# Last stage of a two-block transformer kernel: spilled columns, column order, look-ahead and engine of the elementwise work changed

## The chip, the cores and the metric

The kernel runs on one core of a Trainium2 chip. The metric is the device time of one execution in microseconds, as the median of several runs; lower is better.

## The reference, cut to what matters

The whole program is two transformer blocks on 512 tokens of width 1024. The change concerns the last part of the second block, a layer of 16384 experts (128 columns of 128), of which every token takes 8 x 16:

```
def block(xb):
    q = (xb @ w_query).reshape(T, 8, 2, 128)
    s = einsum('thpk,hpnk->thpn', q, sub_keys)
    top_s, top_i = top_k(s, 16)
    ...
    idx = ...                       # 16 experts per head and token
    gate = softmax(best_s)
    u = expert_u[idx]
    v = expert_v[idx]
    act = gelu(einsum('td,thkd->thk', xb, u))
    return einsum('thk,thkd->td', gate * act, v)
```

After it `x = x + gate2 * peer(...)` and a last rms norm with a weight follow.

## The kernel before, in words

Everything is kept in float32. A product is made of three matmuls on a high and a low part of each operand (`mm3`, L204). `unit` (L189) loads 128 x 1024 weights into one of three `raw` buffers with a DMA that SyncE issues, ScalarE copies them to `whi` (L200), and VectorE or another engine that is handed in subtracts (`wlo`, L201). `whi` and `wlo` have eight buffers each.

The first 128 tokens take their experts by gathering rows (`gather`, L1063): for each of 128 slots GpSimd issues an indirect DMA of 128 rows of 4 KB into one of four `grow` buffers, VectorE makes a dot product with `h2` (L1075), and later a second gathered row is accumulated into `acc0` (L1077). That is 256 gathers of 512 KB.

The other 384 tokens take all 16384 experts, by columns. For a column j, `expert_in` (L1054) multiplies the tokens with the column's `p_u` (24 matmuls of 384 columns) and takes the gelu into `act`. In the last stage, `experts_out` (L1212), `parts` multiplies `act` with the dense gates of the column (L1249), which an earlier stage left in DRAM (`gD`) and which come back as tiles of 4 columns, makes a high and a low part `wh`, `wl` (L1253, L1254), and `prod` multiplies these with the column's `p_v` (18 matmuls of 512 columns: 3 token tiles, 2 halves, `mm3`) into six banks that sum over all columns.

Of the 128 columns 64 (j < `NSPILL`) have their `act` made in the routing stage before, where TensorE waits for VectorE's top-k; they are stored in DRAM (`actD`, L1047) and loaded again in the last stage (`acts`, L1244, two buffers). They are *spilled*; the others are *fresh* and go through `expert_in` in the last stage. The last stage takes a fresh and a spilled column in turn (64, 0, 65, 1, ...). The fresh columns' `wlo` and all gate products are GpSimd's.

The program is written in this order, and then a list scheduler of the language puts each engine's instructions into an order of its own, by simulated times; buffers and semaphores are set after it. On an engine, and in SyncE's queue of loads, instructions then run strictly in that order, so that one which waits holds up those behind it.

Of the kernel before, what the change touches and what calls it, by code (L numbers as in the profile page):

```python
# [18 lines left out]
S = 512  # L19
# [7 lines left out]
NSPILL = 64  # L27
F1 = 4
# [13 lines left out]
# ---------------------------------------------------------------- constants of the shapes  # L42
# [55 lines left out]
# ---------------------------------------------------------------- layout of the inputs  # L98
# [72 lines left out]
# ---------------------------------------------------------------- the program  # L171
class Block:
# [15 lines left out]
    # ---- streams of weights  # L188
# [55 lines left out]
    def to_T(self, src, tt, kt, hh, hl, psp):  # L244
        """128 tokens' rows (features on the free axis) into the transposed pair."""
# [10 lines left out]
    def norm_T(self, np_, psp, tt, wrow):  # L256
        """rms norm of the residual's rows of token tile tt, weighted, into hT."""
# [38 lines left out]
    def post_norm(self, np_, tt, ps, wrow):  # L296
        """x += rms(ps) * w"""
# [8 lines left out]
    # ---- whole  # L306
    def run(self, upto=99):
# [7 lines left out]
        self.x = base.tile([128, NT, D], F32, name="x")  # L315
        nc.sync.dma_start(self.x[:, 0, :], a["x"][:128, :])
        self.hh = base.tile([128, 8, S], F32R, name="hh")
        self.hl = base.tile([128, 8, S], F32R, name="hl")
        self.hhF = self.hh.bitcast(F32)
# [3 lines left out]
        self.oml = base.tile([128, 4], F32, name="oml")  # L323
        self.psum = ctx.enter_context(tc.tile_pool(name="psum", bufs=1, space=PSUM))
# [15 lines left out]
    # ---- block 1, mixer  # L340
# [27 lines left out]
    def rope(self, T, psp, ps, C, Sg, dst, scale=1.0):  # L368
        """dst: a tile, or a pair of tiles that get one half of the partitions each"""
# [74 lines left out]
    def project_nsa(self, P, T, psp, cos, sin):  # L444
# [19 lines left out]
        # hl[:, h]: both parts of head h's queries, one on each half of the partitions;  # L464
        # hh[:, 4 * part + 2 * g + n]: one part of group g's keys, on both halves
# [120 lines left out]
    def attend(self, T, psp):  # L586
# [4 lines left out]
        for tt in range(NT - 1, -1, -1):  # L591
# [5 lines left out]
            # compressed keys  # L597
# [88 lines left out]
    # ---- block 1, conv ffn; the modulation of block 2 rides along  # L686
# [142 lines left out]
    def lower_bounds(self, pool):  # L829
        """the forget gates' lower bounds lb and 1 - lb, a column per head"""  # L830
# [12 lines left out]
    def hgrn(self, P, T, psp, ya, yb):  # L843
# [5 lines left out]
        # projections that the recurrence needs first  # L849
# [25 lines left out]
        # values and output gates, tokens on the partitions  # L875
# [41 lines left out]
    def hgrn_head(self, h, T, psp, tag, kT, qT, b, vv, ya, hm):  # L917
# [27 lines left out]
        # pairs of different token tiles; queries and keys decayed to the tiles' borders  # L945
# [75 lines left out]
    # ---- block 2, experts: token tile 0 gathers its rows, the other tiles take every expert  # L1021
    def peer(self):
# [3 lines left out]
        with ExitStack() as c0:  # L1026
            dr = c0.enter_context(tc.tile_pool(name="pdr", bufs=1, space=DRAM))
            self.actD = dr.tile([128, 128, n], F32, name="actD")
# [5 lines left out]
            with ExitStack() as c1:  # L1034
# [134 lines left out]
    def gates_dense(self, psp, sel, iota):  # L1169
        """the gate of every expert and token, tokens innermost, in DRAM"""  # L1170
# [41 lines left out]
    def experts_out(self):  # L1212
        tc, nc, a = self.tc, self.nc, self.a
        n = S - 128
        last = 4
        with ExitStack() as c0:
# [6 lines left out]
            early = {j: self.expert_in(T, psp.only("pre"), j, nc.gpsimd) for j in range(NSPILL, NSPILL + 3)}  # L1223
            acc = [[psp.tile([128, 512], F32, name="acc") for h in range(2)] for t in range(NT - 1)]
            fresh, spilled = list(range(NSPILL, 128)), list(range(NSPILL))
            order = []
            while fresh or spilled:
                if fresh:
                    order.append(fresh.pop(0))
# [126 lines left out]
```

## Time and profile before

| | |
|---|---|
| runs | 2371.37, 2372.2, 2373.32 us, median 2372.2 |
| span of the profiled execution | 2374.4 us (the page has no time of its own beside it) |
| TensorE busy | 2250.5 us (95%) |
| VectorE busy | 1732.7 us (73%) |
| ScalarE busy | 954.2 us (40%) |
| GpSimd busy | 1191.4 us (50%) |
| last stage | from about 1497 us to the end |

Busy times are sums over stages with different limits, so shares of the whole span tell little of one stage. DVE is VectorE, ACT is ScalarE, POOL is GpSimd, SPq is SyncE's queue that issues loads; PE is TensorE and PEld its weight loads. A matmul's duration in the profile is longer than its share of the pipe, since matmuls overlap; the pace is read from one start to the next. DMA share is the mean busy share of 16 DMA engines.

### The profile page before, as it was taken

The numbers are of one execution on the slowest core, as the hardware profiler recorded it, in microseconds if no ns is written. First come the engines' busy times: TensorE is split into PE (matmuls) and PEld (weight loads), VectorE is DVE, ScalarE is ACT, GpSimd is POOL, SyncE is SP. The second block draws the span as 40 slices with busy tenths as digits, with TensorE's granted clock in tenths as the row PEclk, the third lists the DMA queues.
The fourth block names the chain that finished last, engine by engine and source line by source line (L and its number), as shares of the span: only waits on it lengthen the run. The fifth ranks groups of instructions, "written<-read, shape, count | busy, mean of one in ns | idle before, by whom it ended". The sixth has DMA issues, their size and how long they took to land.

```text
span 2374.4 us, 32466 instructions
## 1 busy us (share of the span) xinstructions
PE 2250.5 (95%) x11849; PEld 1974.4 (83%) x11849; DVE 1732.7 (73%) x2873; ACT 954.2 (40%) x1540; POOL 1191.4 (50%) x811
## 2 busy tenths in 40 slices
PE   7998999999999999999998999899999999999996
PEld 6786878888889888798998999788888788888885
DVE  4347557886425487546599999488888899888898
ACT  4225444333326433433333599423333333333331
POOL 3234110000002233312468898578788888888886
PEclk9998999999999999999999999999999999999998
DMA  7323006765223211143344466899889899989985
GB/s 250 109 66 115 11 5 226 242 213 195 93 76 119 89 63 46 66 145 106 130 132 158 137 242 248 318 317 335 314 308 317 309 319 324 319 315 308 328 304 197
DMA packets 190480, 469.56 MB, mean 198 GB/s; under 512 B 19056, under 2 KB 87536, under 8 KB 190192
## 3 DMA queue, kind: packets, MB, share of 16 engines
q1 hardware_dynamic: 153456, 333.25, 41.2%
q0 software_dynamic: 36864, 134.23, 16.0%
q8 instruction: 93, 1.52, 0.3%
q14 instruction: 67, 0.55, 0.1%
HBM read 422.31 MB, written 39.85 MB: 195 GB/s over the span
## 4 chain that ended last, share of the span: by engine, by line
PE 55%; DVE 16%; DMA 11%; issue 8%; POOL 7%; ACT 3%; SPq 1%; DVEq 0%; POOLq 0%; ACTq 0%
PE b L206 15%; PE b L207 15%; PE b L208 15%; DMA grow<-in_p_v_dram,eid 4%; DMA grow<-in_p_ur_dram,eid 3%; POOL grow L1072 3%; PE b L1203 3%; DVE wlo L201 2%; DVE wl L1254 2%; POOL wlo L201 2%; DVE grow L1075 1%; DMA raw<-in_p_v_dram 1%; PE b L656 1%; DVE acc L1077 1%; ACT gst L1204 1%
## 5 line engine op out<-in xcount | busy, mean ns | idle before, releaser
L206 PE MATMUL b<-hh,wlo 128*128 128x384 f32 (+2 forms) x1872 | 663.1, 355 | 13.8 <-POOL wlo L201 7.3
L207 PE MATMUL b<-hl,whi 128*128 128x384 f32 (+2 forms) x1872 | 661.3, 354 | 3.6 <-DVE hl L288 3.4
L208 PE MATMUL b<-hh,whi 128*128 128x384 f32 (+2 forms) x1872 | 659.4, 353 | 0.0
L201 POOL TENSOR_TENSOR wlo<-raw,whi 128x1024 fp32r<-128x1024 f32 x143 | 359.2, 2521 | 514.6 <-ACT whi L200 500.8
L200 ACT ACTIVATE whi<-raw 128x1024 fp32r<-128x1024 f32 (+1 forms) x405 | 425.6, 1054 | 441.0 <-PE b L208 182.3
L201 DVE TENSOR_TENSOR wlo<-raw,whi 128x1024 fp32r<-128x1024 f32 x262 | 373.8, 1429 | 212.0 <-ACT whi L200 207.0
L206 PEld LDWEIGHTS b<-hh,wlo 128*128 128x128 f32 x1872 | 354.3, 190 | 45.7 <-POOL wlo L201 8.8
L207 PEld LDWEIGHTS b<-hl,whi 128*128 128x128 f32 x1872 | 355.8, 190 | 33.6 <-DVE hl L288 3.8
L208 PEld LDWEIGHTS b<-hh,whi 128*128 128x128 f32 x1872 | 355.0, 190 | 30.1 <-issue 0.4
L206 PE MATMUL b<-whi,wl 128*128 128x512 f32 x768 | 308.4, 402 | 43.7 <-DVE wl L1254 43.7
L207 PE MATMUL b<-wlo,wh 128*128 128x512 f32 x768 | 305.3, 398 | 0.0
L208 PE MATMUL b<-whi,wh 128*128 128x512 f32 x768 | 304.2, 397 | 0.0
L1075 DVE CUSTOM_DVE_ANT_0 grow<-grow,h 128x1024 f32<-128x1024 f32 x128 | 211.3, 1668 | 33.1 <-DMA grow<-in_p_ur_dram,eid 33.0
L1077 DVE SCALAR_TENSOR_TENSOR acc<-grow,gact,acc 128x1024 f32<-128x1024 f32 x127 | 216.0, 1701 | 22.5 <-DMA grow<-in_p_v_dram,eid 20.5
L1072 POOL DMA_INDIRECT grow<-in_p_v_dram,eid x128 | 193.4, 1511 | 75.1 <-DVE acc L1077 39.8
L1072 POOL DMA_INDIRECT grow<-in_p_ur_dram,eid x128 | 196.1, 1532 | 65.8 <-DVE gact L1075 41.0
L206 PEld LDWEIGHTS b<-whi,wl 128*128 128x128 f32 x768 | 147.5, 192 | 80.6 <-DVE wl L1254 50.9
L206 PE MATMUL b<-whi,hl 128*128 128x512 f32 (+1 forms) x464 | 181.6, 392 | 4.4 <-DVE hl L254 2.3
L208 PE MATMUL b<-whi,hh 128*128 128x512 f32 (+1 forms) x464 | 180.1, 388 | 0.0
L207 PE MATMUL b<-wlo,hh 128*128 128x512 f32 (+1 forms) x464 | 180.0, 388 | 0.0
L208 PEld LDWEIGHTS b<-whi,wh 128*128 128x128 f32 x768 | 148.1, 193 | 31.9
L207 PEld LDWEIGHTS b<-wlo,wh 128*128 128x128 f32 x768 | 148.3, 193 | 29.6
(296 smaller groups left out, 3093.6 us busy)
## 6 DMA issues: line engine op xcount, KB each, us to landing
raw<-in_p_u_dram SPq DMA_DIRECT2D x128, 512.0 KB
raw<-in_p_v_dram SPq DMA_DIRECT2D x128, 512.0 KB
raw<-in_w_adaT_dram SPq DMA_DIRECT2D x48, 512.0 KB
gD<-gst SPq DMA_DIRECT2D x48, 512.0 KB
raw<-in_w_up_dram SPq DMA_DIRECT2D x44, 512.0 KB
raw<-in_w_t_dram SPq DMA_DIRECT2D x32, 512.0 KB
gtf<-gD SPq DMA_DIRECT2D x16, 768.0 KB
gt<-gD SPq DMA_DIRECT2D x16, 768.0 KB
```

The costliest lines, as they stand in the source:

```text
L200: nc.scalar.activation(hi, raw, AF.Copy)
L201: (eng or nc.vector).tensor_tensor(lo, raw, hi.bitcast(F32), op=ALU.subtract)
L206: mm(out, al, bh, start=start, stop=False)
L207: mm(out, ah, bl, start=False, stop=False)
L208: mm(out, ah, bh, start=False, stop=stop)
L656: nc.tensor.matmul(po[:, i, :], pT[:, b, :], self.vv[:, b, 128 * br + 64 * g:128 * br + 64 * g + 64], start=b == 0, stop=b == tt)
L1072: nc.gpsimd.indirect_dma_start(out=g, out_offset=None, in_=rows[n], in_offset=bass.IndirectOffsetOnAxis(ap=self.eid[:, s:s + 1], axis=0))
L1075: nc.vector.tensor_tensor_reduce(g, g, self.h2, 1.0, 0.0, ALU.mult, ALU.add, act[:, s:s + 1])
L1077: nc.vector.scalar_tensor_tensor(self.acc0, g, act[:, s:s + 1], self.acc0, op0=ALU.mult, op1=ALU.add)
L1203: nc.tensor.matmul(ps[:, i, :], A[:, i, :], B[:, i, :], start=True, stop=True)
L1204: nc.scalar.activation(st.rearrange("p j t -> p t j")[:, 4 * t4:4 * t4 + 4, :], ps, AF.Copy)
L1254: nc.vector.tensor_tensor(wl, act, wh.bitcast(F32), op=ALU.subtract)
```

## The change

All of it is in `experts_out`, in the number of the columns that the routing stage spills, and in the order in which the base pool's tiles are made; comments and docstrings go as well, by which lines shift by up to two, and by four to five in `experts_out`.

- Spilled columns are the even ones, fresh the odd ones; the last stage takes 0, 1, 2, ... `actD` is half as long.
- Gate tiles hold 8 columns: 16 loads of 1536 KB instead of 32 of 768 KB.
- `parts` is written two columns ahead of `prod` (`AHEAD = 2`).
- The fresh columns' `wlo` and all gate products are VectorE's; GpSimd keeps the gathers' issues and small work at the end.
- `acts` has three buffers instead of two.
- In the base pool `x` comes behind `hh` and `hl`, which changes addresses.

```diff
+AHEAD = 2
...
-        self.x = base.tile([128, NT, D], F32, name="x")
-        nc.sync.dma_start(self.x[:, 0, :], a["x"][:128, :])
-        self.hh = base.tile([128, 8, S], F32R, name="hh")
...
+        self.hh = base.tile([128, 8, S], F32R, name="hh")
+        self.hl = base.tile([128, 8, S], F32R, name="hl")
+        self.hhF = self.hh.bitcast(F32)
+        self.x = base.tile([128, NT, D], F32, name="x")
+        nc.sync.dma_start(self.x[:, 0, :], a["x"][:128, :])
...
-            self.actD = dr.tile([128, 128, n], F32, name="actD")
+            self.actD = dr.tile([NSPILL, 128, n], F32, name="actD")
...
-                            act = self.expert_in(self.gpool or Q, psp, j, nc.gpsimd, "ga" if self.gpool else "act")
+                            act = self.expert_in(self.gpool or Q, psp, 2 * j, nc.gpsimd, "ga" if self.gpool else "act")
...
-            early = {j: self.expert_in(T, psp.only("pre"), j, nc.gpsimd) for j in range(NSPILL, NSPILL + 3)}
+            early = {j: self.expert_in(T, psp.only("pre"), j, nc.vector) for j in (1, 3, 5)}
...
-                g, jj = j // 4, j % 4
+                g, jj = j // 8, j % 8
...
-                    gts[g] = T.tile([128, 12, 4, 32], F32, name="gt" if g < NSPILL // 4 else "gtf")
+                    gts[g] = T.tile([128, 12, 8, 32], F32, name="gt")
...
+                if j % 2 == 0:
+                    act = T.tile([128, n], F32, name="acts", bufs=3)
+                    nc.sync.dma_start(act, self.actD[j // 2])
+                elif j in early:
+                    act = early.pop(j)
+                else:
+                    act = self.expert_in(T, psp, j, nc.vector)
                 v = self.unit(a["p_v"][j])
...
-                nc.gpsimd.tensor_tensor(act.rearrange("p (c t) -> p c t", t=32), act.rearrange("p (c t) -> p c t", t=32),
+                nc.vector.tensor_tensor(act.rearrange("p (c t) -> p c t", t=32), act.rearrange("p (c t) -> p c t", t=32),
...
-            for n_, j in enumerate(order[:-last]):
-                p = parts(j)
+            ready = [parts(j) for j in range(AHEAD)]
+            for j in range(128 - last):
+                ready.append(parts(j + AHEAD))
+                p = ready.pop(0)
```

The scheduler leaves every engine's order as it was up to the last stage. In it, TensorE's order before is this (a number at a name is the buffer's; `b4` and `b5` are the banks of `expert_in`, `b0` to `b7` else the sums; `wl_16586` belongs to the gelu of `b4_16557`, `wl_16696` to that of `b5_16667`):

```order
L208 MATMUL b4_16557<-hh_66,whi_16553 128x384
L206 MATMUL b5_16667<-hh_66,wlo_16664 128x384
...
L208 MATMUL b5_16667<-hh_66,whi_16663 128x384
L206 MATMUL b0_13317<-whi_16547,wl_16586 128x512
...
L208 MATMUL b7_13322<-whi_16615,wh_16622 128x512
L206 MATMUL b4_16774<-hh_66,wlo_16771 128x384
...
L206 MATMUL b0_13317<-whi_16657,wl_16696 128x512
```

The first `...` stands for the rest of 24 matmuls, the second for 36 of two columns, the third for the rest of 5. And now, at the same depth (`wl_16454` belongs to the product before `b4_16524`, `wl_16559` to `b4_16524`):

```order
L207 MATMUL b4_16524<-hh_68,wlo_16521 128x384
...
L209 MATMUL b4_16524<-hh_68,whi_16520 128x384
L207 MATMUL b0_13317<-whi_16448,wl_16454 128x512
...
L209 MATMUL b7_13322<-whi_16485,wh_16490 128x512
L207 MATMUL b5_16631<-hh_68,wlo_16628 128x384
...
L209 MATMUL b5_16631<-hh_68,whi_16627 128x384
L207 MATMUL b0_13317<-whi_16553,wl_16559 128x512
```

The products of an expert are no longer in pieces of 19, 24 and 5 but in 24s, each followed by 36 of two columns, and a column's first product has moved from behind the next expert to behind two columns and the next expert.

VectorE's order in the same place before (`acc0` rows are the gather's):

```order
L201 TENSOR_TENSOR wlo_16765<-raw_16762,whi_16764 128x1024
L1077 SCALAR_TENSOR_TENSOR acc0_8232<-grow_16220,gact_13198,acc0_8232 128x1024
L1077 SCALAR_TENSOR_TENSOR acc0_8232<-grow_16287,gact_13198,acc0_8232 128x1024
L1254 TENSOR_TENSOR wl_16586<-act_16582,wh_16585 128x384
L1254 TENSOR_TENSOR wl_16623<-acts_16619,wh_16622 128x384
L201 TENSOR_TENSOR wlo_16833<-raw_16830,whi_16832 128x1024
```

and now:

```order
L1079 SCALAR_TENSOR_TENSOR acc0_8232<-grow_16302,gact_13198,acc0_8232 128x1024
L1245 TENSOR_TENSOR act_16549<-act_16549,gt_16161 128x384
L1079 SCALAR_TENSOR_TENSOR acc0_8232<-grow_16305,gact_13198,acc0_8232 128x1024
L1250 TENSOR_TENSOR wl_16559<-act_16549,wh_16558 128x384
L1250 TENSOR_TENSOR wl_16598<-acts_16588,wh_16597 128x384
L202 TENSOR_TENSOR wlo_16701<-raw_16698,whi_16700 128x1024
L202 TENSOR_TENSOR wlo_16736<-raw_16733,whi_16735 128x1024
L1079 SCALAR_TENSOR_TENSOR acc0_8232<-grow_16370,gact_13198,acc0_8232 128x1024
L202 TENSOR_TENSOR wlo_16769<-raw_16766,whi_16768 128x1024
```

The gate product (L1245) and the fresh column's `wlo` (here `wlo_16736`) have come into VectorE's queue, between the gathered rows, of which it still takes four per two columns.

## Rows read from the trace of the kernel before

**Rows 1.** Stretches of the last stage: busy time by engine, clock, DMA share, GB/s
```profile
core 0: us, PE busy (x) PEld busy (x) DVE busy (x) ACT busy (x) POOL busy (x), PEclk, DMA share, GB/s
1515.00:2315.00 800.00, 760.40 (x3566) 663.43 (x3565) 692.12 (x609) 265.74 (x367) 650.44 (x419) 0.98 0.91 317
```
**Rows 2.** Timeline of TensorE: start us, duration us, instruction
```profile
1802.29 0.39 PE L208 MATMUL b<-whi,wh 128*128 128x512 f32 x1
...
1807.73 0.39 PE L208 MATMUL b<-whi,wh 128*128 128x512 f32 x1
...
1807.96 0.34 PE L208 MATMUL b<-hh,whi 128*128 128x384 f32 x1
...
1812.73 0.34 PE L208 MATMUL b<-hh,whi 128*128 128x384 f32 x1
```
**Rows 3.** Groups of instructions on TensorE, 1515 to 2315 us
```profile
line engine op names shapes xcount | busy us, mean ns | idle before us <-releasers
L206 PE MATMUL b<-whi,wl 128*128 128x512 f32 x724 | 290.2, 401 | 36.8 <-DVE wl L1254 36.8
...
L206 PE MATMUL b<-hh,wlo 128*128 128x384 f32 x465 | 158.1, 340 | 2.8 <-POOL wlo L201 2.8
```
**Rows 4.** Waits from 1500 us to the end: total us, times, longest
```profile
PE b L206 <- DVE wl L1254: 43.7, 21, 6.9
```
**Rows 5.** Timelines of VectorE and GpSimd, two places
```profile
1787.84 2.73 DVE L1254 TENSOR_TENSOR wl<-act,wh 128x384 fp32r<-128x384 f32 x1
1790.49 0.55 DVE L1254 TENSOR_TENSOR wl<-acts,wh 128x384 fp32r<-128x384 f32 x1
...
1808.63 1.21 DVE L201 TENSOR_TENSOR wlo<-raw,whi 128x1024 fp32r<-128x1024 f32 x1
1809.79 1.32 DVE L1077 SCALAR_TENSOR_TENSOR acc<-grow,gact,acc 128x1024 f32<-128x1024 f32 x1
...
1787.58 2.57 POOL L201 TENSOR_TENSOR wlo<-raw,whi 128x1024 fp32r<-128x1024 f32 x1
...
1807.77 1.78 POOL L1072 DMA_INDIRECT grow<-in_p_v_dram,eid  x1 [0.16 <-issue]
1809.86 0.94 POOL L1072 DMA_INDIRECT grow<-in_p_v_dram,eid  x1 [0.30 <-DVE wlo L201]
```
**Rows 6.** Groups of instructions on VectorE, 1515 to 2315 us
```profile
L1075 DVE CUSTOM_DVE_ANT_0 grow<-grow,h 128x1024 f32<-128x1024 f32 x125 | 206.8, 1672 | 33.1 <-DMA grow<-in_p_ur_dram,eid 33.0
L201 DVE TENSOR_TENSOR wlo<-raw,whi 128x1024 fp32r<-128x1024 f32 x118 | 195.6, 1660 | 21.3 <-ACT whi L200 21.2
L1077 DVE SCALAR_TENSOR_TENSOR acc<-grow,gact,acc 128x1024 f32<-128x1024 f32 x111 | 190.8, 1719 | 15.9 <-DMA grow<-in_p_v_dram,eid 14.1
L1254 DVE TENSOR_TENSOR wl<-act,wh 128x384 fp32r<-128x384 f32 x62 | 66.3, 1069 | 26.4 <-ACT wh L1253 20.9 <-ACT whi L200 3.0 <-issue 2.5
L1254 DVE TENSOR_TENSOR wl<-acts,wh 128x384 fp32r<-128x384 f32 x61 | 54.6, 895 | 6.6 <-ACT wh L1253 6.6
L1075 DVE DVE_READ_ACCUMULATOR2_ANT gact<- 128x1 f32 x124 | 9.5, 77 | 0.0
```
**Rows 7.** One line of VectorE, the gather's dot product: duration ns min/median/max
```profile
L1075 DVE CUSTOM_DVE_ANT_0 grow<-grow,h x128: 1207/1217/4919, 1503.7 to 2319.7; 128x1024 f32<-128x1024 f32 x128
```
**Rows 8.** Waits of SyncE's queue from 1500 us to the end
```profile
SPq L1244 <- DVE wl L1254: 235.3, 57, 10.4
...
SPq L192 <- POOL wlo L201: 171.7, 37, 6.3
```
**Rows 9.** Two stretches of 100 us in the stage, columns as in rows 1
```profile
1500.00:1600.00 100.00, 91.77 (x425) 80.03 (x425) 68.99 (x69) 31.46 (x45) 69.36 (x47) 0.97 0.94 331
...
1900.00:2000.00 100.00, 97.00 (x468) 85.53 (x468) 90.86 (x79) 33.48 (x46) 83.90 (x54) 1.00 0.94 327
```
**Rows 10.** DMA queues from 1500 us to the end: packets, MB, share of 16 engines
```profile
q1 hardware_dynamic: 86672, 136.86, 45.4%
q0 software_dynamic: 36705, 133.65, 43.2%
```
**Rows 11.** Timeline of VectorE at the start of the stage
```profile
1518.35 0.78 DVE L1254 TENSOR_TENSOR wl<-act,wh 128x384 fp32r<-128x384 f32 x1 [13.44 <-ACT wh L1253]
```
**Rows 12.** Waits from 2300 us to the end
```profile
PE b L206 <- DVE wl L1254: 7.5, 2, 6.9
```

More of the change, by code (lines that the diff above doesn't have):

```diff
@@ L314, in run @@
         nc.vector.memset(self.ones, 1.0)
-        self.x = base.tile([128, NT, D], F32, name="x")
-        nc.sync.dma_start(self.x[:, 0, :], a["x"][:128, :])
-        self.hh = base.tile([128, 8, S], F32R, name="hh")
-        self.hl = base.tile([128, 8, S], F32R, name="hl")
-        self.hhF = self.hh.bitcast(F32)
         self.mod = base.tile([128, 48], F32, name="mod")
@@ L1222, in experts_out @@
             g2 = self.gate_row(P, psp.only("u"), 40, "g2")
-            early = {j: self.expert_in(T, psp.only("pre"), j, nc.gpsimd) for j in range(NSPILL, NSPILL + 3)}
+            early = {j: self.expert_in(T, psp.only("pre"), j, nc.vector) for j in (1, 3, 5)}
             acc = [[psp.tile([128, 512], F32, name="acc") for h in range(2)] for t in range(NT - 1)]
[L1225 to L1229, printed above, removed]
-                if len(spilled) * (128 - NSPILL) > len(fresh) * NSPILL or not fresh:
-                    if spilled:
-                        order.append(spilled.pop(0))
@@ L1241, in parts @@
-                v = self.unit(a["p_v"][j])
-                if j < NSPILL:
-                    act = T.tile([128, n], F32, name="acts", bufs=2)
-                    nc.sync.dma_start(act, self.actD[j])
-                elif j in early:
-                    act = early[j]
-                else:
-                    act = self.expert_in(T, psp, j, nc.gpsimd)
-                nc.gpsimd.tensor_tensor(act.rearrange("p (c t) -> p c t", t=32), act.rearrange("p (c t) -> p c t", t=32),
+                                      self.gD[:, :, 256 * g:256 * g + 256].rearrange("c i n -> i c n"))
@@ L1255, in parts, with prod @@
                 return v, wh, wl
-            def prod(n_, t, v, wh, wl, halves=(0, 1)):
+            def prod(j, t, v, wh, wl, halves=(0, 1)):
                 tok = slice(128 * t, 128 * t + 128)
@@ L1260, in prod @@
                     c = slice(512 * h, 512 * h + 512)
-                    self.mm3(acc[t][h], wh[:, tok], wl[:, tok], v[0][:, c], v[1][:, c], n_ == 0, n_ == 127)
+                    self.mm3(acc[t][h], wh[:, tok], wl[:, tok], v[0][:, c], v[1][:, c], j == 0, j == 127)
             def finish(tt, src):
@@ L1277, in experts_out @@
             done = 0
-            for n_, j in enumerate(order[:-last]):
-                p = parts(j)
+            ready = [parts(j) for j in range(AHEAD)]
+            for j in range(128 - last):
+                ready.append(parts(j + AHEAD))
+                p = ready.pop(0)
                 for t in range(NT - 1):
-                    prod(n_, t, *p)
-                goal = min(257, 257 * (n_ + 1) // GBY)
+                    prod(j, t, *p)
+                goal = min(257, 257 * (j + 1) // GBY)
                 _advance(gather, goal - done)
@@ L1285, in experts_out @@
             _advance(gather, 999)
-            ps = [parts(j) for j in order[-last:]]
+            ready += [parts(j) for j in range(128 - last + AHEAD, 128)]
             finish(0, [self.acc0[:, :512], self.acc0[:, 512:]])
@@ L1289, in experts_out @@
                 for h in range(2):
-                    for i, p in enumerate(ps):
+                    for i, p in enumerate(ready):
                         prod(128 - last + i, t, *p, halves=(h,))
```

1 line of the change is left out of this document (removed).

## The prediction

> **What bounds the kernel now.** I read the stretches first, since one core runs four stages with different limits. The change moves no instruction ahead of the last stage, so only the time from about 1497 us on matters; the rest is taken as it is. There [rows 1], the 800 us from 1515 to 2315 are a steady state in which three resources are near full together: TensorE busy 760, VectorE 692, the DMA engines at a share of 0.91 (317 GB/s). GpSimd is at 650, ScalarE at 266. A share of 95% on TensorE says little, so I next work out what its matmuls need.
>
> The pace is read from starts [rows 2]. From 1802.29 to 1807.73 lie 24 steps of 512-wide matmuls, 0.2267 us each; from 1807.96 to 1812.73 lie 27 steps of 384-wide ones, 0.1767 us. The stretch holds 2170 of the first and 1396 of the second (three lines of nearly equal count each [rows 3]): 491.9 + 246.7 = **738.6 us of work in 800**. So 61.4 us are lost. Idle waits are 36.8 + 2.8 = 39.6 of them [rows 3]; the other 22 go with a mean granted clock of 0.98 [rows 1], that is, mostly 2.4 GHz with pieces at 1.2 after waits. That is all that can be won in the stretch.
>
> Next, who ends those waits. Nearly all of the idle is one sort: the first product of a column (L1261) waits for its `wl` [rows 4]. Its making is ScalarE's gelu, the product with the gate (L1249, GpSimd), ScalarE's copy `wh` and VectorE's `wl`. Two things make it late. First, TensorE's order gives every second column little room: as the order section shows, only the 24 matmuls of the next expert, 24 x 0.1767 = 4.2 us, lie between the last matmul behind `wl_16586` and its use; the other column has 41 matmuls, 36 x 0.2267 + 5 x 0.1767 = 9.0 us. Second, VectorE jams. The rows of one place show it [rows 5]: `wl` took 2.73 us at 1787.84 with GpSimd's 2.57 us subtraction beside it, and 0.55 at 1790.49 without one. The subtraction `wlo` took 1.21 and the accumulation 1.32 while GpSimd issued a gather; the issue does not slow them. The means over the stretch, 1672, 1660, 1719, 1069 and 895 ns [rows 6], against a median of 1217 for the gather's dot product [rows 7], tell that this is common.
>
> Last, the queue that issues loads: SyncE stood 235.3 us in total at the load of `acts` until `wl` set its buffer free, and 171.7 at loads of `raw` until GpSimd's `wlo` did [rows 8]. Behind a load that stands, all later ones stand too.
>
> **The change, part by part.**
>
> *GpSimd's work to VectorE.* In the stretch GpSimd loses about 59 subtractions and 123 gate products; VectorE gains them. With nobody beside it I price its work at the undisturbed durations: 125 dot products x 1.217 = 152; 125 reads of the accumulator x 0.077 = 10 [rows 6]; 118 + 59 = 177 subtractions x 1.21 = 214; 111 accumulations x 1.32 = 147; 123 `wl` x 0.55 = 68; 123 gate products of the same 128x384 shape, taken like `wl`, 68. Sum **659 us**, against 206.8 + 195.6 + 190.8 + 66.3 + 54.6 + 9.5 = 724 now. The added 139 us are more than paid by the jams that go. The gate product is not shown on VectorE; its ends are 0.55 (as `wl`) and 1.21 (as the 1024-wide subtraction), 81 us more and 740 in all. I take 0.55, the same size and two inputs.
>
> The Trainium skill, "Perfetto Trace Analysis", section "Optimizing Scalar/DVE Operations", speaks against this part: a saturated VectorE may be relieved by ScalarE or even GpSimd, which is what the kernel before does; the same section warns that the two share a read port, so that it might not help. The rows of group 5 side with the warning; by the rule alone the sum is that of rival 4.
>
> *Parts two columns ahead.* TensorE's new order is 24 matmuls for an expert, 36 for two products, 24, 36. Between the last matmul behind `wl_16559` and its use lie 36 + 24 matmuls, 12.4 us, against 4.2 and 9.0. Gelu, product, copy and `wl` follow within that even if VectorE is some us late. The cover for this is the weights' eight buffers; no third column of loads is needed beyond them.
>
> *`acts` with three buffers instead of two* takes part of the 235.3 us of standing out of SyncE's queue, and raw buffers come free with VectorE's 1.21 instead of GpSimd's 2.57 us. Both let loads start earlier, and what is then late is the DMA itself.
>
> *What loads can give.* The same bytes at the pure matmul pace need a share of 0.91 x 800 / 738.6 = 0.986. The best hundred microseconds in the stage show 0.94 [rows 9], with 0.92 of PE busy in one and 0.97 at clock 1.00 in the other. I take 0.94 as what better supplied queues reach all along: 800 x 0.91 / 0.94 = 774.5 us.
>
> *Gate tiles of 8.* Two loads of 768 KB become one of 1536 KB, with runs of 1 KB instead of 512 B: 24576 packets instead of 32 x 12 x 128 = 49152. Their price lies in [rows 10]: GpSimd's queue, nearly all 4 KB rows, moved 133.65 MB in 43.2%, 3.094 MB per percent. At that rate the other queue's 136.86 MB would be 44.2%, not 45.4: all short packets together cost 1.2% of 874 us, 10 us. Half of that, 5 us, is the gain (ends 0 and 10). So 774.5 - 5 = **769.5**, a gain of 30.5. The Trainium skill, "DMA: Bandwidth & Descriptors", section "Specifications", puts line rate at 512 B and above; by it this term would be 0, not 5.
>
> *TensorE's own side* would give less time: the better of the hundred-us rows is 97% busy [rows 9], 738.6 / 0.97 = 761.4. The later of the two, 769.5, is the forecast for the stretch.
>
> *Start.* The first product now is a spilled column that needs gate tile and `acts`; before, a fresh one, whose `wl` came at 1518.35 [rows 11]. Three gate products and one more `wh`/`wl` precede it on VectorE, 3 x 0.55 + 0.55 + 0.5, and its load follows the tile's: 0 to 5 us, taken as 2.
>
> *End.* TensorE waits up to 6.9 us there for the last columns' `wl` [rows 12]. Behind VectorE's last gathered rows it can stay or go: 0 to -7, taken as -4.
>
> *Spilled columns even, natural order, base pool:* the same 64 columns are spilled with the same loads and stores, only others; addresses move. 0, as VectorE's median of 1217 ns over four rotating buffers shows no place that is slower; ends 0 and 2 us either way.
>
> Sum: -30.5 + 2 - 4 = -32.5. The profiled execution's span is 2374.4 us, and 2341.9 comes of it. The median of the runs is 2372.2, 2.2 below the span, so **2340 us**.
>
> **The rivals.**
>
> 1. *The DMA stays where it is.* Four gather buffers and three raw buffers are unchanged, and 0.91 may be their limit. Then only the gate tiles and the end count, 5 + 4 - 2: 2365. For it: 0.91 is a mean over 800 us; against it: SyncE's standing [rows 8] is time with free engines. 0.14.
> 2. *All waits go.* The stretch falls to 738.6, with start 0 and end -7: -68, 2304. Against it: the share of 0.986. 0.08.
> 3. *VectorE's queue takes the place of GpSimd's (slower).* Everything that feeds TensorE now stands in one order with the gathered rows. Its waits in the stretch are 33.1 + 15.9 for rows, 21.3 + 26.4 + 6.6 for ScalarE's copies [rows 6], 103 in all. With 659 of work it fills 762; at 800 the change loses, so it decides at waits of 141, a third more. If they double, 659 + 206 = 865, less 2 at the ends: 2372 + 63 = 2435; half more gives 2384. Loads that start earlier speak against it. 0.11.
> 4. *The moved work keeps its stretched durations*, the skill's rule of above: 724 + 59 x 1.66 + 123 x 0.98 = 943 on VectorE, 143 more than the stretch: 2515. Only if the jams were not GpSimd's; [rows 5] speak against it. 0.03.
> 5. *Gains and new waits cancel*, within 0.2% (5 us, what a measurement of this kernel can tell from no change). 0.07.
>
> **How the numbers follow.** My forecast, 2315 to 2355, holds 0.57. Faster by over 0.2%: 0.57 + 0.14 + 0.08 = 0.79; same 0.07; slower 0.14. The range 2310 to 2372 leaves out rivals 3 and 4, most of 2 and half of 5. It takes in the ends of gate product, tiles, start and end.
>
> **What would show it.** VectorE's `wlo` and dot product near 1.21 us in the mean, the gate product at 0.55; idle of TensorE before `wl` below 10 us in the steady state; a DMA share of 0.94 or more; clock near 1.00; no SyncE wait on GpSimd. Wrong would be: means that stay above 1.5 us; VectorE over 95% busy with TensorE still waiting for `wl`; a DMA share of 0.91 with raw loads as the last wait (rival 1).

## The result, and the profile after

The changed kernel takes **2302.99 us** (median of four runs, 2300.91 to 2311.13) against 2372.76 us (2371.37 to 2382.8) of the kernel before, run beside it: a ratio of 0.9706 [0.9682, 0.9731], 69.8 us less. The prediction was 2340 with a range from 2310 to 2372; the time lies 7 us below the range, at the price of rival 2 (2304). The profiled execution is the longest of the four, 2311.13 us with a span of 2309.4.

The changed kernel's stretches of the last stage, columns as in [rows 1]:

```profile
1515.00:2215.00 700.00, 697.32 (x3355) 614.31 (x3356) 569.94 (x738) 250.10 (x343) 301.89 (x223) 0.99 0.94 340
1600.00:1700.00 100.00, 100.00 (x487) 88.46 (x486) 83.03 (x107) 35.79 (x49) 44.26 (x33) 1.00 0.96 348
2000.00:2100.00 100.00, 100.00 (x486) 88.28 (x485) 81.90 (x107) 37.11 (x51) 44.93 (x32) 1.00 0.92 338
```

From 1600 on TensorE is never without work and the granted clock is 1.00; [rows 1] had 95% and 0.98. The DMA share went from 0.91 to 0.94, the bytes from 317 to 340 GB/s.

The changed kernel's waits of TensorE, 1500 us to the end (total us, times, longest); they answer to [rows 4, 12]:

```profile
PE b L207 <- DVE wl L1250: 13.1, 1, 13.1
PE b L207 <- DVE wlo L202: 2.8, 1, 2.8
```

Both happen once, at the start of the stage. The 39.6 us of idle in the steady state [rows 3] are gone, and so is the wait at the end.

VectorE's groups in the changed kernel, 1515 to 2215 us, columns as in [rows 6]:

```profile
L202 DVE TENSOR_TENSOR wlo<-raw,whi 128x1024 fp32r<-128x1024 f32 x166 | 200.5, 1220 | 23.7 <-ACT whi L201 23.4
L1079 DVE SCALAR_TENSOR_TENSOR acc<-grow,gact,acc 128x1024 f32<-128x1024 f32 x111 | 142.0, 1279 | 4.4 <-DMA grow<-in_p_v_dram,eid 3.5
L1077 DVE CUSTOM_DVE_ANT_0 grow<-grow,h 128x1024 f32<-128x1024 f32 x111 | 133.8, 1219 | 2.2 <-DMA grow<-in_p_ur_dram,eid 2.0
L1245 DVE TENSOR_TENSOR acts<-acts,gt 128x384 f32<-128x384 f32 x60 | 33.2, 553 | 3.6 <-DMA acts<-actD 3.6
L1250 DVE TENSOR_TENSOR wl<-acts,wh 128x384 fp32r<-128x384 f32 x59 | 32.6, 552 | 5.5 <-ACT wh L1249 5.5
L1250 DVE TENSOR_TENSOR wl<-act,wh 128x384 fp32r<-128x384 f32 x58 | 32.1, 553 | 8.0 <-ACT wh L1249 8.0
L1245 DVE TENSOR_TENSOR act<-act,gt 128x384 f32<-128x384 f32 x55 | 30.7, 557 | 82.7 <-ACT act L1062 82.6
```

The means are what single undisturbed instructions were before [rows 5, 7]: 1220 ns for `wlo`, 1279 for the accumulation, 1219 for the dot product and 553 for the fresh column's `wl`, against 1660, 1719, 1672 and 1069 [rows 6]. The gate product, new on VectorE, takes 553 and 557. VectorE has taken over a third kind of work and is busy 81% of the stretch instead of 87%. The 82.6 us in the last row are spare time: the gelu it waits for follows TensorE.

SyncE's queue, 1500 us to the end (compare [rows 8]):

```profile
SPq L193 <- DVE wlo L202: 343.0, 154, 6.9
SPq L1239 <- DVE wl L1250: 175.4, 53, 7.4
```

[rows 8] leave out the wait that answers to the first of these. The kernel before:

```profile
SPq L192 <- DVE wlo L201: 191.6, 100, 5.9
```

So the queue stood 235.3 + 191.6 + 171.7 = 598.6 us for these buffers before and stands 518.4 us now, nearly all of it on VectorE. That is not much less, and it costs nothing: from 1518 us on TensorE waits for nothing.

### The profile page after: what moved, and what is told of

Read it like the earlier page. It is cut to its first block, busy times and chain, and to the rows that moved or that the text cites. A ratio compares the mean times of both kernels' runs of the same rounds, so it can differ in the third digit from the quotient of the medians.

```text
span 2309.4 us, 32140 instructions
## 1 busy us (share of the span) xinstructions
PE 2211.4 (96%) x11849; PEld 1959.7 (85%) x11849; DVE 1645.3 (71%) x3065; ACT 955.0 (41%) x1540; POOL 841.4 (36%) x619
## 5 line engine op out<-in xcount | busy, mean ns | idle before, releaser
L207 PE MATMUL b<-hh,wlo 128*128 128x384 f32 (+2 forms) x1872 | 656.1, 352 | 10.7 <-ACT act L1062 5.5
L208 PE MATMUL b<-hl,whi 128*128 128x384 f32 (+2 forms) x1872 | 654.2, 350 | 3.9 <-DVE hl L289 3.3
L202 DVE TENSOR_TENSOR wlo<-raw,whi 128x1024 fp32r<-128x1024 f32 (+1 forms) x326 | 396.8, 1226 | 216.5 <-ACT whi L201 211.4
L202 POOL TENSOR_TENSOR wlo<-raw,whi 128x1024 fp32r<-128x1024 f32 x79 | 199.6, 2540 | 494.9 <-ACT whi L201 485.6
L207 PE MATMUL b<-whi,wl 128*128 128x512 f32 x768 | 299.9, 390 | 13.1 <-DVE wl L1250 13.1
L1074 POOL DMA_INDIRECT grow<-in_p_ur_dram,eid x128 | 170.7, 1334 | 249.7 <-DVE gact L1077 173.1
L1074 POOL DMA_INDIRECT grow<-in_p_v_dram,eid x128 | 175.3, 1370 | 208.4 <-DVE acc L1079 131.2
L1062 ACT ACTIVATE act<-b 128x384 f32<-128x384 f32 x114 | 55.8, 491 | 351.3 <-PE b L209 315.3
L1079 DVE SCALAR_TENSOR_TENSOR acc<-grow,gact,acc 128x1024 f32<-128x1024 f32 x127 | 162.5, 1280 | 6.9 <-DMA grow<-in_p_v_dram,eid 5.7
```

What stands on the lines that cost most here:

```text
L202: (eng or nc.vector).tensor_tensor(lo, raw, hi.bitcast(F32), op=ALU.subtract)
L207: mm(out, al, bh, start=start, stop=False)
L208: mm(out, ah, bl, start=False, stop=False)
L1062: self.nc.scalar.activation(act, ps, AF.Gelu)
L1074: nc.gpsimd.indirect_dma_start(out=g, out_offset=None, in_=rows[n], in_offset=bass.IndirectOffsetOnAxis(ap=self.eid[:, s:s + 1], axis=0))
L1079: nc.vector.scalar_tensor_tensor(self.acc0, g, act[:, s:s + 1], self.acc0, op0=ALU.mult, op1=ALU.add)
```

## Experiments: which part gave the gain

The four kernels of this group (each against the kernel before, run beside it):

| kernel | median us | ratio |
|---|---|---|
| `before_dve` | 2309.7 | 0.9736 [0.9711, 0.976] |
| `before_base` | 2356.57 | 0.9931 [0.991, 0.9952] |
| `before_dve_base` | 2295.54 | 0.9679 [0.9663, 0.9696] |
| `base_back` | 2319.57 | 0.9773 [0.9752, 0.9794] |

`before_dve` is the kernel before with one part of the change, GpSimd's elementwise work on VectorE:

```diff
-            early = {j: self.expert_in(T, psp.only("pre"), j, nc.gpsimd) for j in range(NSPILL, NSPILL + 3)}
+            early = {j: self.expert_in(T, psp.only("pre"), j, nc.vector) for j in range(NSPILL, NSPILL + 3)}
...
-                nc.gpsimd.tensor_tensor(act.rearrange("p (c t) -> p c t", t=32), act.rearrange("p (c t) -> p c t", t=32),
+                nc.vector.tensor_tensor(act.rearrange("p (c t) -> p c t", t=32), act.rearrange("p (c t) -> p c t", t=32),
```

and the same for the later fresh columns. Expected:

> The kernel before with VectorE doing GpSimd's subtractions and gate products, nothing else. Theory 1 (jams): wlo and dot product fall to 1.22 us in the mean, idle before wl from 44 to under 20 us: 2335 to 2350 us. Theory 2 (room in TensorE's order): idle before wl stays over 30 us: 2360 to 2372. Theory 3 (VectorE's queue takes GpSimd's place): slower than 2376.

Measured: 2309.7, so this part alone is worth 62 us, nearly the whole gain, with the old order of columns, no look-ahead, tiles of 4 and two `acts` buffers. It isn't the engines alone, though: the scheduler, given other times, also sets TensorE's instructions anew. The room of 4.2 us, which 23 of the 64 fresh columns have in the kernel before, is left to 13 here. Both come with this edit, and no run separates them.

`before_base` is the kernel before with only the base pool's new order, `base_back` the changed kernel with the old one (the diff of the base pool that stands with the change, alone, forwards and backwards). Expected of `before_base`:

> The kernel before with the base pool's new order alone. Theory of the address: the conv ffn gains 8 us, the last stage's TensorE work 5 us of which waits take some back: 2358 to 2364 us. Rival (chance): 2372 within 3.

Expected of `base_back`:

> The changed kernel with the base pool in its former order, x ahead of hh and hl, so that hh starts at byte 192 of a 512-byte line again instead of 0. Theory (the address of the moving operand sets TensorE's pace): matmuls of 512 tokens step 0.233 us again instead of 0.227, those of 384 step 0.177 instead of 0.173, those of 256 step 0.113 instead of 0.120; the conv ffn between 440 and 720 us takes 8 us more, the last stage 5 us more: 2313 to 2318 us. Rival (the earlier stages differ by chance, addresses do nothing): 2303, paces as in the changed kernel.

Measured: `before_base` takes 15 us less than the kernel before that ran beside it (16 by the ratio), `base_back` 16.6 us more than the changed kernel (16 by the ratios). A part that I had priced at nothing is worth some 16 us.

`before_dve_base` has both parts and nothing else. Expected:

> The kernel before with two parts of the change alone: GpSimd's subtractions and gate products to VectorE, and the base pool's new order. If the two add up (61.8 and 14.9 us were measured apart), 2294 to 2298 us, faster than the whole change (2303), and then column order, look-ahead, tiles of 8 and the third acts buffer together cost some 7 us. Rival (the address gain was waiting time that is gone once TensorE is always busy, or the DMA is now the bound): 2303 to 2310.

Measured: 2295.54, the best kernel of the study, 7 us below the changed kernel. The two parts add up; what else the change holds costs 7 us by the medians. The intervals of the two ratios overlap, but the profiles show where such a loss lies: TensorE's wait at the start is 3.9 us here and 13.1 in the changed kernel. Its steady state, columns as in [rows 1]:

```profile
1515.00:2215.00 700.00, 700.00 (x3393) 617.95 (x3392) 573.86 (x742) 251.93 (x345) 296.29 (x227) 1.00 0.95 344
```

TensorE is full here too, without `AHEAD`.

## Experiment: what in the base pool

`hh192` is the changed kernel with `hh` and `hl` 320 bytes lower, which puts them at 192 in a line of 512 bytes, as before; `x`, the weights and all behind stay.

```diff
+        self.hh = base.tile([128, 8, S], F32R, name="hh")
+        self.hl = base.tile([128, 8, S], F32R, name="hl")
         self.mod = base.tile([128, 48], F32, name="mod")
...
-        self.hh = base.tile([128, 8, S], F32R, name="hh")
-        self.hl = base.tile([128, 8, S], F32R, name="hl")
```

Expected:

> The changed kernel with only hh and hl moved by 320 bytes (ahead of four tiny tiles instead of behind them): they start at 192 in a line of 512 bytes, as before the change, while x, the weights and all else lie where the change put them. If the place of TensorE's moving operand is the cause of the base pool's 15 us: the step of 512-token matmuls goes from 0.227 back to 0.233 us, that of 384 tokens in the last stage from 0.173 to 0.177, that of 256 tokens from 0.120 to 0.113, and the time to 2315 to 2321. If x's place (VectorE's and the DMA's) is the cause: steps as in the changed kernel or no difference in time, 2303 within 4 us.

Measured: 2319.94 us, 0.9781 [0.9752, 0.981], the time of `base_back`. The pace is shown by 960 matmuls in a row with `hh` or `hl` as moving operand and 512 columns, in the conv ffn of block 1; first and last on TensorE's timeline (start us, duration us, instruction). The kernel before:

```profile
379.81 0.39 PE L206 MATMUL b<-hh,wlo 128*128 128x512 f32 x1
...
603.57 0.40 PE L208 MATMUL b<-hh,whi 128*128 128x512 f32 x1
```

The changed kernel:

```profile
386.59 0.40 PE L207 MATMUL b<-hh,wlo 128*128 128x512 f32 x1
...
603.99 0.39 PE L209 MATMUL b<-hh,whi 128*128 128x512 f32 x1
```

`hh192`:

```profile
381.33 0.39 PE L207 MATMUL b<-hh,wlo 128*128 128x512 f32 x1
...
605.09 0.40 PE L209 MATMUL b<-hh,whi 128*128 128x512 f32 x1
```

Over 959 steps: 223.76 us or 0.2333 each, 217.40 or 0.2267, and 223.76 or 0.2333 again. One place gives 6.4 us. The durations of single matmuls (0.39, 0.40) do not show it; only the starts do. With 384 columns in the last stage the step is 0.177 at 192 [rows 2] and 0.174 at 0. With 256 columns the sign turns: the run of 199 that begins at 738.85 in the changed kernel has a mean step of 0.1204, in `hh192` and before (from 740.87 and 741.41) 0.1182. `x` keeps its new place in `hh192`, so it isn't the cause of these steps.

The moving operand is not the whole of it. In the 464 matmuls right behind, `hh` and `hl` are the stationary operand, and the moving one is the weights, which lie where they were. There the step is 0.2333 us in the kernel before (603.80 to 711.84 us), 0.2289 in `hh192` (605.32 to 711.31) and 0.2267 in the changed kernel (604.22 to 709.17), 3.1 us more of the 16. Why it has three values stays open. Whether the line of 512 bytes or another unit counts, and what other offsets do, wasn't tried.

## Experiments: why GpSimd's work costs so much

Five kernels give back to GpSimd all or a part of what the change took from it; all else is the changed kernel.

| kernel | GpSimd's again | median us | ratio |
|---|---|---|---|
| `wlo_pool` | fresh columns' `wlo` | 2308.92 | 0.9739 [0.9718, 0.9761] |
| `mul_pool` | all gate products | 2307.93 | 0.973 [0.9711, 0.9749] |
| `half_acts` | `wlo`, spilled products | 2316.46 | 0.9787 [0.977, 0.9805] |
| `half_pool` | `wlo`, fresh products | 2347.63 | 0.9894 [0.9869, 0.9919] |
| `gpsimd_back` | `wlo`, all products | 2379.07 | 1.003 [1.0014, 1.0046] |

The edits are these lines, alone or together (`half_pool` and `half_acts` choose the engine by `j % 2`):

```diff
-                    act = self.expert_in(T, psp, j, nc.vector)
+                    act = self.expert_in(T, psp, j, nc.gpsimd)
...
-                nc.vector.tensor_tensor(act.rearrange("p (c t) -> p c t", t=32), act.rearrange("p (c t) -> p c t", t=32),
+                nc.gpsimd.tensor_tensor(act.rearrange("p (c t) -> p c t", t=32), act.rearrange("p (c t) -> p c t", t=32),
```

**gpsimd_back.** Expected:

> The changed kernel with GpSimd doing the fresh columns' subtraction and all gate products again. Theory 1 (VectorE's jams beside GpSimd were the cause): wlo and dot product rise to 1.6 us in the mean, VectorE is over 90% busy, TensorE waits for wl again: 2325 to 2345 us. Theory 2 (the room of 12.4 us between an expert and its use is enough by itself): durations rise just so, but TensorE hardly waits: 2303 to 2310.

Measured: 2379 us, 0.3% slower than the kernel before, and 22.5 us slower than `before_base`, which has the same engines and the same base pool. Look-ahead, natural order, tiles and buffers together do not help where GpSimd keeps its work, they hurt; which of them does was not tried. Waits from 1515 to 2340 us:

```profile
ACT wh L1249 <- POOL act L1245: 370.2, 59, 10.0
DVE wl L1250 <- ACT wh L1249: 136.4, 57, 3.7
...
PE b L207 <- DVE wl L1250: 47.4, 32, 4.4
```

TensorE waits for `wl` 32 times, although 12.4 us of other matmuls now lie ahead of each use. The first row leads back: ScalarE stands at `wh` for GpSimd's product, once per pair of columns. One such pair on GpSimd's timeline:

```profile
1939.38 0.94 POOL L1074 DMA_INDIRECT grow<-in_p_ur_dram,eid  x1 [0.30 <-DVE gact L1077]
1940.34 2.40 POOL L202 TENSOR_TENSOR wlo<-raw,whi 128x1024 fp32r<-128x1024 f32 x1
1942.90 1.76 POOL L1074 DMA_INDIRECT grow<-in_p_ur_dram,eid  x1 [0.16 <-issue]
1944.97 1.96 POOL L1074 DMA_INDIRECT grow<-in_p_ur_dram,eid  x1 [0.30 <-issue]
1946.95 1.02 POOL L1245 TENSOR_TENSOR act<-act,gt 128x384 f32<-128x384 f32 x1
```

and on ScalarE's:

```profile
1938.68 0.47 ACT L1062 ACTIVATE act<-b 128x384 f32<-128x384 f32 x1
1940.31 1.06 ACT L201 ACTIVATE whi<-raw 128x1024 fp32r<-128x1024 f32 x1 [1.16 <-DMA raw<-in_p_v_dram]
1948.00 0.52 ACT L1249 ACTIVATE wh<-act 128x384 fp32r<-128x384 f32 x1 [6.63 <-POOL act L1245]
...
1948.85 1.04 ACT L201 ACTIVATE whi<-raw 128x1024 fp32r<-128x1024 f32 x1
```

The gelu is done at 1939.2. Its product comes at 1946.95, behind a gather's issue, a subtraction of 2.40 us and two more issues. ScalarE stands for it 6.63 us, and behind `wh` stands `whi`, the copy that the next weights and their raw buffers need.

**wlo_pool and mul_pool** take the two kinds of work apart. Expected of `wlo_pool`:

> The changed kernel with only the fresh columns' subtraction on GpSimd again (64 of 2.5 us, 160 us of GpSimd), gate products on VectorE. Theory P (VectorE is blocked beside GpSimd's elementwise work, cost in proportion to its time, 160 of the 295 us that cost 76): 2335 to 2350. Theory Q (the gate products stand in GpSimd's queue behind gathers' issues that wait for VectorE): under 2315.

Expected of `mul_pool`:

> The changed kernel with only the gate products on GpSimd again (128 of 1.05 us, 135 us of GpSimd), subtraction on VectorE. Theory P: 2330 to 2345. Theory Q: 2360 to 2380, with TensorE waiting for wl and ScalarE's wh waiting for GpSimd's product.

Measured: 5.9 and 4.9 us over the changed kernel (the intervals overlap with its own), where both together cost 76. Neither theory as written there gives that. TensorE is at 100% from 1515 to 2215 in both, though VectorE's means are longer beside GpSimd (the accumulation 1629 ns in `wlo_pool`, 1316 in `mul_pool`): jams alone do not stop TensorE.

**half_pool** was to tell a queue at its limit (theory R) from two kinds of work that disturb each other (theory I). Expected:

> The changed kernel with the fresh columns' subtraction and the fresh columns' gate product on GpSimd; the spilled columns' products stay on VectorE. Each kind alone cost 5 to 6 us, both 76. Theory R (GpSimd's queue in order is a loop at its limit: once its work fits between the gathered rows, it has slack): GpSimd busy about 302 + 151 + 66 = 519 of the 700 us from 1515 to 2215, against 549 where all is its work and PE falls behind, 449 to 461 where one kind is; TensorE stays near 100% there and the time is at most 2320. Theory I (the two kinds disturb each other, and the cost grows with the product of both amounts): 2303 + 6 + 2.5 + 65 / 2 = 2344, with TensorE at about 95% and waits for wl through the whole stretch.

Measured: 2347.63, where theory I put it and far over R's 2320, with GpSimd busy only 500 of the 700 us. R fell. But TensorE did not wait through the whole stretch, as I had it: of 27 us lost there most come in single waits some 52 us apart, between stretches without any. (Some 15 us more are lost at the end, where the gathered rows come last.) TensorE's waits from 1515 to 2215 us:

```profile
PE b L207 <- POOL wlo L202: 12.2, 6, 4.1
PE b L207 <- DVE wl L1250: 5.4, 4, 3.2
```

Most of them are for the weights' low part on GpSimd, not for `wl`. A gate tile is loaded every 50 to 55 us, once for 8 columns, and each of the six waits of over 1 us from 1515 us on ends 24 to 29 us after such a load's issue. The loads around a gate tile seem to have a part in it; `half_pool` with smaller tiles was not tried.

A third theory, S, was formed from ScalarE's rows, and **half_acts**, same kinds and amount of work but the other half of the products, was to tell it from I. Expected:

> The changed kernel with the fresh columns' subtraction and the spilled columns' gate product on GpSimd; the fresh columns' products stay on VectorE. It is the run of 2347.6 us with the other half of the products: same kinds, same amount of GpSimd work. Theory S (ScalarE, in order, stands at wh until GpSimd has the fresh column's product, which lies behind a subtraction of 2.6 us and gather issues that wait for VectorE; its slack, seen as its wait for TensorE at the gelu, goes from 247 us to 222, 124, 22 and 7 in the runs of 2303, 2309, 2308, 2348 and 2379 us): the spilled column's product waits for no gelu and is mostly done in time, ScalarE keeps over 100 us of that slack between 1515 and 2215, and the time is at most 2315. Theory I (the amount of both kinds decides): 2340 to 2350 again.

Measured: 2316.46, 31 us less than `half_pool` (25 by the ratios, since the two ran beside different executions of the kernel before), with TensorE at 100% in the stretch and GpSimd busier (533 us). Theory I fell. S has its slack of over 100 us (106.1 below) and misses its time by 1.5 us; what it did not foresee is that ScalarE stands 148.5 us at `wh` for VectorE's product. What it reads are two rows of ScalarE's groups, 1515 to 2215 us (busy, mean ns, idle before and what ended it). The changed kernel:

```profile
L1249 ACT ACTIVATE wh<-act 128x384 fp32r<-128x384 f32 x57 | 29.8, 522 | 28.1 <-DVE act L1245 22.9 <-PE b L209 5.2
...
L1062 ACT ACTIVATE act<-b 128x384 f32<-128x384 f32 x54 | 26.6, 492 | 246.7 <-PE b L209 246.7
```

`mul_pool`:

```profile
L1249 ACT ACTIVATE wh<-act 128x384 fp32r<-128x384 f32 x56 | 29.4, 525 | 133.2 <-POOL act L1245 128.1 <-PE b L209 5.1
...
L1062 ACT ACTIVATE act<-b 128x384 f32<-128x384 f32 x54 | 26.4, 488 | 124.1 <-PE b L209 124.1
```

`half_acts`:

```profile
L1249 ACT ACTIVATE wh<-act 128x384 fp32r<-128x384 f32 x57 | 30.0, 526 | 152.2 <-DVE act L1245 148.5 <-PE b L209 3.7
...
L1062 ACT ACTIVATE act<-b 128x384 f32<-128x384 f32 x55 | 26.7, 486 | 106.1 <-PE b L209 106.1
```

`half_pool`:

```profile
L1249 ACT ACTIVATE wh<-act 128x384 fp32r<-128x384 f32 x55 | 28.9, 525 | 286.2 <-POOL act L1245 282.0 <-PE b L209 4.2
...
L1062 ACT ACTIVATE act<-b 128x384 f32<-128x384 f32 x52 | 24.9, 478 | 22.1 <-PE b L209 22.1
```

`gpsimd_back`:

```profile
L1249 ACT ACTIVATE wh<-act 128x384 fp32r<-128x384 f32 x52 | 27.3, 525 | 316.2 <-POOL act L1245 311.0 <-PE b L209 5.1
...
L1062 ACT ACTIVATE act<-b 128x384 f32<-128x384 f32 x50 | 23.7, 474 | 7.2 <-PE b L209 7.2
```

The lower row of each pair is ScalarE's slack, the time it waits for TensorE's results. What ScalarE stands at `wh` is taken from it, roughly one for one: 247, 124, 106, 22, 7. In this order, where TensorE has 12.4 us of other work ahead of each use, the steady state loses nothing as long as some is left; when it is used up, TensorE waits. A product behind issues alone costs a wait of 2.3 us per column (128.1 / 56), one behind a subtraction as well 5.1 (282.0 / 55). That fits two cheap halves that make a dear whole.

The slack does not tell it for every order. The kernel before has 114.1 us of it in the same 700, more than `half_acts`, and loses 7% of its pace all the same:

```profile
L1060 ACT ACTIVATE act<-b 128x384 f32<-128x384 f32 x50 | 24.4, 487 | 114.1 <-PE b L208 114.1
```

There the room in TensorE's order is short; the trace of it stands with "Parts two columns ahead" below.

## Experiments: the rest of the change

Three kernels take single parts out of the changed kernel:

```diff
-AHEAD = 2
+AHEAD = 0
```

is `no_ahead`. Expected:

> The changed kernel with parts written in the same turn as the products (AHEAD 0). The prediction's step, that the room of 12.4 us in TensorE's order is worth tens of us, expects waits before wl in the steady state again: 2320 to 2345. Theory that VectorE's undisturbed work is enough by itself: 2295 to 2308, no waits in the steady state.

Measured: 2299.27, 0.969 [0.967, 0.971], no more than with it (the intervals overlap). TensorE's waits for `wl` from 1480 us on are 14.7 us, 12.7 of them in one piece at the start and 2.0 in the steady state. Look-ahead is worth nothing once VectorE makes the products, although the scheduler leaves 7 of the 64 fresh columns the room of 4.2 us here.

```diff
-                    act = T.tile([128, n], F32, name="acts", bufs=3)
+                    act = T.tile([128, n], F32, name="acts", bufs=2)
```

is `acts2`. Expected:

> The changed kernel with two buffers for acts instead of three. If the third buffer was needed (SyncE stood 235 us at these loads before): SyncE's wait at acts grows, loads behind it come late and TensorE waits for whi or wl; over 2310. If it was not (TensorE at 100% has cover of two columns): 2303 within 4 us. A kernel without look-ahead and with two buffers already had 2295 to 2310, which speaks for the second.

Measured: 2299.94, 0.9698 [0.9674, 0.9721]. The third buffer is worth nothing either.

```diff
-                g, jj = j // 8, j % 8
+                g, jj = j // 4, j % 4
...
-                    gts[g] = T.tile([128, 12, 8, 32], F32, name="gt")
+                    gts[g] = T.tile([128, 12, 4, 32], F32, name="gt", bufs=4)
```

is `gt4`, with loads of 128 rows to match. Expected:

> The changed kernel with gate tiles of 4 columns (four buffers) as before. If the first tile's 1536 KB set the 13 us that TensorE waits at the start of the stage: that wait falls to about 5 us and the time to 2295; the 512-byte packets cost nothing visible, since the DMA has room at TensorE's full pace. If the short packets matter, the prediction's 5 us (0 to 10) are lost in the steady state and TensorE falls below 100% there: 2303 to 2308. If the wait is set by the order of the columns (a spilled one first), it stays at 13 us: 2303.

Measured: 2307.49, 0.9732 [0.9699, 0.9765]: no gain, though the wait at the start fell from 13.1 to 6.1 us as the first case has it, and TensorE is at 100% from 1515 to 2215. The first of these rows is GpSimd's at the end of `gt4`, the second TensorE's last matmul:

```profile
2287.68 2.48 POOL L1264 TENSOR_TENSOR acc<-acc,g 128x512 f32<-128x512 f32 x2 [10.30 <-DVE acc L1079]
...
2281.02 0.39 PE L209 MATMUL b<-whi,wh 128*128 128x512 f32 x1
```

The same two of the changed kernel:

```profile
2292.08 2.55 POOL L1264 TENSOR_TENSOR acc<-acc,g 128x512 f32<-128x512 f32 x2 [4.59 <-DVE acc L1079]
...
2295.68 0.39 PE L209 MATMUL b<-whi,wh 128*128 128x512 f32 x1
```

In the changed kernel the gathered rows are summed 3.6 us ahead of TensorE's end. In `gt4` they are 6.7 us behind it, and the 24 us from the last matmul to the end of the span (2304.9) are theirs, against 13.7. What the start gave, the end took: the gathered rows are the next bound. The same holds for `half_acts` (their sum at 2294.16, the last matmul at 2283.60) and `wlo_pool` (2289.00 and 2283.1), so what these two cost lies there and not in the steady state.

## Why the prediction was wrong

**What holds.** The first step: 738.6 us of need in 800, of which 61.4 can be won. All of it was won but the start: in the seven hundred us above TensorE lacks 2.7. The diagnosis that GpSimd's elementwise work makes VectorE jam holds, with the durations to 0.05 us. The Trainium skill, "SBUF — State Buffer", section "Who interferes with whom", has the rule that a VectorE instruction with two SBUF inputs contends with a GpSimd one that reads SBUF. The traces agree: 1.66 us in the mean with such work beside it, 1.22 with gather issues alone.

**The step that failed** is "What loads can give": the same bytes at the full pace need a share of 0.986, 0.94 is what queues reach, hence 774.5 us and -30.5. Full pace needed 317 x 800 / 738.6 = 343 GB/s, and the changed kernel moves 340 at a share of 0.94, `before_dve_base` 344 at 0.95. So 0.94 was the right share and the wrong conclusion: share and bytes do not go together in a fixed ratio. The stretch gave 59 us, not 30.5. The changed kernel's queues, 1500 us to the end (packets, MB, share; compare [rows 10]):

```profile
q1 hardware_dynamic: 61415, 135.28, 46.6%
q0 software_dynamic: 36290, 132.14, 44.5%
```

The gathered rows are the same 4 KB packets as before and took 0.432 x 874.4 / 133.65 = 2.83 us of the share per MB before and 0.445 x 809.4 / 132.14 = 2.73 now. In `gpsimd_back` it is 2.83 again (131.61 MB, 42.5% of 877.3 us). `half_acts` and `wlo_pool`, at full pace with part of GpSimd's work, have 2.76 and 2.77. Over all kernels it is 2.83 to 2.85 where GpSimd has all of its elementwise work (`before_base` too), 2.76 to 2.78 where it has a part (`mul_pool` and `half_pool` too), and 2.71 to 2.75 where it has none. So a packet's time is not fixed and goes with GpSimd's work; why stays open. And TensorE's waits before were for `wl` [rows 4], not for weights: a share that was never seen to stop it was no ceiling to multiply with. The whole case against rival 2 stood in that one sentence on 0.986.

**A second step failed, and it took the time out of the range:** the base pool's addresses at 0, with ends at 2 us. `base_back`, which is the change without that part, takes 2319.57 us, 20 below the forecast and inside the range. The part itself is worth some 16 us. I argued its 0 with VectorE's median and never looked at TensorE, whose operands `hh` and `hl` had moved.

**Parts two columns ahead** was given as what makes `wl` timely. It was not: with 12.4 us of room and GpSimd's work, TensorE waits 32 times; with less room and with VectorE (`before_dve_base`, `no_ahead`), hardly at all. The chain from gelu to `wl` became short.

In the order before, that chain was longer than its room. At the place of [rows 5], ScalarE, GpSimd and TensorE of the kernel before:

```profile
1784.85 0.49 ACT L1060 ACTIVATE act<-b 128x384 f32<-128x384 f32 x1 [5.71 <-PE b L208]
1785.42 1.02 POOL L1249 TENSOR_TENSOR act<-act,gtf 128x384 f32<-128x384 f32 x1 [1.01 <-ACT act L1060]
1786.47 0.52 ACT L1253 ACTIVATE wh<-act 128x384 fp32r<-128x384 f32 x1
...
1790.62 0.50 PE L206 MATMUL b<-whi,wl 128*128 128x512 f32 x1 [1.57 <-DVE wl L1254]
```

The gelu starts at 1784.85, and `wl`, which takes 2.73 us beside GpSimd's subtraction, is done at 1790.57. That is 5.7 us where the next expert gives 4.2, and TensorE waits 1.57 us. From 1515 to 2215 us the time from a gelu's start to the end of its column's `wl` is 5.6 us in the mean of 50 columns. In `before_dve` it is 3.5 us over 55 columns, and TensorE waits for none of them after the start. So short room and a chain made long by VectorE's jam and GpSimd's product did make `wl` late, as the prediction has it; only the room is short in 23 of 64 columns and not in every second one. How much of the cure is the shorter chain and how much the scheduler's new order stays open for `before_dve`; from the changed kernel to `gpsimd_back` the order of the 24 and 36 matmuls stays, and there it is GpSimd's work alone.

**acts with three buffers:** credited with part of 235.3 us of SyncE's standing; worth nothing (`acts2`). The standing was not what was late.

**Gate tiles of 8:** 5 us. As DMA time that is right: 46.6% of 804.9 us for 132.16 MB in `gt4`, 2.84 us per MB, against 0.466 x 809.4 / 135.28 = 2.79, or 6.6 us over the stage. (Kernels with tiles of 8 and VectorE's products lie between 2.76 and 2.79, so it is rough.) In time it is worth nothing, as the DMA bounds nothing.

**Start:** +2, measured 13.1 us in one wait against 3.9 in `before_dve_base`: 9. I counted VectorE's instructions and left out the load itself. The first tile is issued at 1496.57 and ends VectorE's wait 15 us later:

```profile
1511.51 1.50 DVE L1245 TENSOR_TENSOR act<-act,gt 128x384 f32<-128x384 f32 x3 [10.32 <-DMA gt<-gD]
...
1517.08 0.55 DVE L1250 TENSOR_TENSOR wl<-acts,wh 128x384 fp32r<-128x384 f32 x1
```

(VectorE's timeline of the changed kernel.) **End:** -4; the wait of 7.5 us is gone, but from the last matmul to the end it is 13.7 us now and 11.4 before (2363.0 to 2374.4), so -5.

Put together: -59 in the steady state, -5 at the end, +9 at the start and -16 from the base pool make -71, against -69.8 measured. Rival 2 had the steady state right. That its price of -68 hits the time is partly luck, since it has neither the start nor the base pool, which make -7 together.

**Rivals 3 and 4:** VectorE's waits did not double. Those of rows and copies in [rows 6] were 103 us in 800; the answering ones above are 44 in 700 (the wait for the gelu, 82.6, is spare time), and 569.94 us of work leave room for them. The Trainium skill, "Perfetto Trace Analysis", section "Optimizing GPSIMD Operations", advises other engines than GpSimd where possible. Here that is worth 62 us alone, with VectorE already at 87%.

## What to carry to other kernels

An engine in order that stands for a helper passes the wait on to all that is queued behind it. Read two things before giving the helper more: the room that the bound engine's order leaves for the chain through the helper, and the slack of the engine that stands (its idle time that the bound engine ends). With 12.4 us of room the cost was near nil until the slack was used up, and steep from there; with 4.2 us it came with slack left. Do not turn a DMA share into a ceiling by proportion; ask for the GB/s that the full pace needs and whether any load is the last thing waited for. Price a moved address by looking at every engine that reads it. And when a wait is removed, look at what ends next: here the gathered rows, by which a sound repair of the start (`gt4`) brought nothing.

## What was not expected of the hardware

- The place of `hh` and `hl` in SBUF goes with the step of the matmuls that read them. As moving operand at 192 in a line of 512 bytes the step is 0.2333 us for 512 columns and at 0 it is 0.2267, for 384 columns 0.177 and 0.174; for 256 columns it is the other way, 0.118 and 0.120. As stationary operand it was 0.2333 and 0.2289 at 192 and 0.2267 at 0. The recorded durations do not show it.
- The DMA engines' busy time per byte is not fixed: 2.83 to 2.85 us of the share per MB for the 4 KB rows while GpSimd does all of its elementwise work, 2.71 to 2.75 without.
